# Grouped-query attention on one core: score matmuls as two 64-row tiles, inputs turned by DMA, and a fifth of the exponentials on VectorE

## The chip, the core and the metric

The kernel runs on one core of a Trainium2 chip. A core has a matrix engine (PE, TensorE) that writes only into PSUM, an activation engine (ACT, ScalarE), a vector engine (DVE, VectorE), a general engine (POOL, GpSimd) and a sync engine (SP) that issues transfers. Data lies in SBUF (128 partitions) and, for matmul results, in PSUM (128 partitions, 8 banks of 512 fp32 columns). Engines run side by side and wait for each other through semaphores. Transfers to and from the main memory (HBM) run on 16 DMA engines; SP and POOL issue them here.

The metric is the device time of one execution in microseconds (us), as the median of several runs.

## The reference: what is computed

Eight batches, eight query heads, two key/value heads, 1024 positions, head size 64. Four query heads share one key/value head.

```python
batch, n_q_heads, n_kv_heads, seq, head_dim = (8, 8, 2, 1024, 64)
...
scale = 1.0 / np.sqrt(head_dim)
for g in range(n_kv_heads):
    ...
    scores = scale * np.matmul(q_group, k_group.transpose(0, 1, 3, 2))
    scores_max = np.max(scores, axis=-1, keepdims=True)
    attn = np.exp(scores - scores_max)
    attn = attn / (np.sum(attn, axis=-1, keepdims=True) + 1e-08)
    output[:, q_start:q_end, :, :] = np.matmul(attn, v_group)
```

All inputs and the output are float32. Entries are about 0.1 in size, so scores are small, and both kernels take exp without subtracting the maximum. In total there are 64 (batch, head) pairs with 1024 x 1024 scores each, so 67 million exponentials: 524,288 for each of the 128 partitions.

## The kernel before

Scores are computed transposed: keys on the partitions, queries along the columns. That way the exponentials come out in the layout that the second matmul needs, and no transpose of the probabilities is needed. A *cell* is 128 keys by 512 queries; three cells make a *wave*, which fills one slot of three PSUM banks. Two such slots exist.

```python
qT_pool = ctx.enter_context(tc.tile_pool(name="qTpool", bufs=2 * NPAIR))
pT_pool = ctx.enter_context(tc.tile_pool(name="pTpool", bufs=16))
...
spool = ctx.enter_context(tc.tile_pool(name="spsum", bufs=2, space=bass.MemoryType.PSUM))
opool = ctx.enter_context(tc.tile_pool(name="opsum", bufs=1, space=bass.MemoryType.PSUM))
tpool = ctx.enter_context(tc.tile_pool(name="tpsum", bufs=1, space=bass.MemoryType.PSUM))
```

Inputs are loaded as fp32. PE transposes them, reading only the upper 16 bits of each value (`_hi16`) as bf16; VectorE copies the result out of PSUM. Two heads are turned together, so the 128 partitions of `qT` hold head 2j in the lower 64 and head 2j+1 in the upper 64. The key tile has zeros in the other half, so that a 128-row matmul gives the scores of one head alone.

```python
def transpose_group(stages, lo, name_pool):
    tp = tpool.tile([128, NSC, 128], BF16, name="tpsum")
    for sc in range(NSC):
        nc.tensor.transpose(tp[:, sc, :], _hi16(stages[sc])[:, lo : lo + 2, :], ident)   # L107
    dst = name_pool.tile([128, NSC, 128], BF16, name="xT")
    nc.vector.tensor_copy(out=dst, in_=tp)                                              # L111
    return dst
```

One wave: three score matmuls, then one exponential over 1536 columns on ACT.

```python
def score_wave(gw, qT, kT):
    ...
    sps = spool.tile([128, CPERW, QBS], FP32, name="spsum")
    with tc.high_priority(offset=1 << 20):
        for slot, gc in enumerate(cells):
            ...
            nc.tensor.matmul(                                                           # L183
                sps[:, slot, :],
                lhsT=kT[b][g][side][:, c, :],
                rhs=qT[(b, pair)][:, qb * NQS : (qb + 1) * NQS, :],
                start=True, stop=True,
            )
    pt = pT_pool.tile([128, CPERW, QBS], BF16, name="pt")
    nc.scalar.activation(out=pt[:, 0:n, :], in_=sps[:, 0:n, :], func=AF.Exp, scale=scale)  # L191
    return pt
```

The output of 512 queries takes 32 matmuls. The value tile has a 65th column of ones, so the sum of the exponentials comes with the output and VectorE divides by it.

```python
def output_block(b, pair, side, qb, pts, vt):
    ops = opool.tile([128, NQS, D + 1], FP32, name="opsum")
    ...
    for qs in range(NQS):
        for c in range(NKC):
            nc.tensor.matmul(ops[:, qs, :], lhsT=..., rhs=_hi16(vt[b][g][:, c, :]),      # L204
                             start=(c == 0), stop=(c == NKC - 1))
    rec = recip_pool.tile([128, NQS], FP32, name="rec")
    nc.vector.reciprocal(out=rec, in_=ops[:, :, D])                                     # L214
    ost = ostage_pool.tile([128, NQS, D], FP32, name="ost")
    nc.vector.tensor_tensor(out=ost, in0=ops[:, :, 0:D], in1=..., op=ALU.mult)          # L216
    (nc.gpsimd if (qb + side) % 2 else nc.sync).dma_start(out=..., in_=ost)             # L222
```

The file also holds a function for exponentials on VectorE (`dve_exp_cell`), which nothing calls. The order of instructions on each engine is left to the scheduler of the language layer, with raised priority for the scores.

Of the kernel before, what the change touches and what calls it, by code (L numbers as in the profile page):

```python
# [10 lines left out]
def _hi16(ap: bass.AP) -> bass.AP:  # L11
    b = ap.bitcast(mybir.dt.bfloat16)
    return b[..., 1::2]
# [3 lines left out]
def kernel(  # L17
# [7 lines left out]
    nc = tc.nc  # L25
    FP32 = mybir.dt.float32
    BF16 = mybir.dt.bfloat16
    AF = mybir.ActivationFunctionType
# [3 lines left out]
    G = k.shape[1]  # L32
    HPG = H // G
    NPAIR = H // 2
    NKC = S // 128
    NSC = S // 128
    QBS = 512
    NQB = S // QBS
    NQS = QBS // 128
    CPERW = 3  # L40
    NCELL = 2 * NQB * NKC
    scale = 1.0 / math.sqrt(D)

    VEC_EVERY = 5
    LOG2E = 1.4426950408889634
    EC2 = 0.2385171
    EHH = 1.47456484
    EMM = 0.48179846

    const_pool = ctx.enter_context(tc.tile_pool(name="constp", bufs=1))  # L50

    qstage_pool = ctx.enter_context(tc.tile_pool(name="qstage", bufs=2 * NSC))
    kstage_pool = ctx.enter_context(tc.tile_pool(name="kstage", bufs=2 * NSC))
    vstage_pool = ctx.enter_context(tc.tile_pool(name="vstage", bufs=2 * G))

    qT_pool = ctx.enter_context(tc.tile_pool(name="qTpool", bufs=2 * NPAIR))
    kT_pool = ctx.enter_context(tc.tile_pool(name="kTpool", bufs=2 * 2 * G))

    pT_pool = ctx.enter_context(tc.tile_pool(name="pTpool", bufs=16))

    ostage_pool = ctx.enter_context(tc.tile_pool(name="ostage", bufs=4))
    recip_pool = ctx.enter_context(tc.tile_pool(name="recip", bufs=4))
    vexp_pool = ctx.enter_context(tc.tile_pool(name="vexp", bufs=2))

    spool = ctx.enter_context(tc.tile_pool(name="spsum", bufs=2, space=bass.MemoryType.PSUM))
    opool = ctx.enter_context(tc.tile_pool(name="opsum", bufs=1, space=bass.MemoryType.PSUM))
    tpool = ctx.enter_context(tc.tile_pool(name="tpsum", bufs=1, space=bass.MemoryType.PSUM))

    ident = const_pool.tile([128, 128], BF16)
    make_identity(nc, ident)  # L70

    def load_stage(b):
        kstage = []
        qstage = []
        for sc in range(NSC):
            ks = kstage_pool.tile([128, 2 * G + 1, D], FP32, name="kstage")
            nc.vector.memset(ks[:, 0::2, :], 0.0)  # L77
            nc.sync.dma_start(
                out=ks[:, 1::2, :],
                in_=k[b].rearrange("g (sc p) d -> sc p g d", p=128)[sc],  # L80
            )
            kstage.append(ks)
            qstage.append(qstage_pool.tile([128, H, D], FP32, name="qstage"))
        for j in range(NPAIR):
            eng = nc.gpsimd if j % 2 == 0 else nc.sync
            for sc in range(NSC):
                eng.dma_start(  # L87
                    out=qstage[sc][:, 2 * j : 2 * j + 2, :],
                    in_=q[b, 2 * j : 2 * j + 2].rearrange(
                        "h (sc p) d -> sc p h d", p=128  # L90
                    )[sc],
                )
        vt = []
        for g in range(G):
            vs = vstage_pool.tile([128, NKC, D + 1], FP32, name="vstage")
            nc.vector.memset(vs[:, :, D], 1.0)  # L96
            nc.sync.dma_start(
                out=vs[:, :, 0:D],
                in_=v[b, g].rearrange("(c p) d -> p c d", p=128),
            )  # L100
            vt.append(vs)
        return qstage, kstage, vt

    def transpose_group(stages, lo, name_pool):
        tp = tpool.tile([128, NSC, 128], BF16, name="tpsum")
        for sc in range(NSC):
            nc.tensor.transpose(  # L107
                tp[:, sc, :], _hi16(stages[sc])[:, lo : lo + 2, :], ident
            )
        dst = name_pool.tile([128, NSC, 128], BF16, name="xT")  # L110
        nc.vector.tensor_copy(out=dst, in_=tp)  # L111
        return dst

    def prologue_transposes(qstage, kstage):
        kT = [[None, None] for _ in range(G)]
        qT = [None] * NPAIR
        order = []
        seen = set()
        for j in range(NPAIR):
            g = (2 * j) // HPG  # L120
            if g not in seen:
                seen.add(g)
                order.append(("k", (g, 0)))
                order.append(("q", j))
                order.append(("k", (g, 1)))
            else:
                order.append(("q", j))
        for kind, idx in order:
            if kind == "k":
                g, side = idx  # L130
                kT[g][side] = transpose_group(kstage, 2 * g + 1 - side, kT_pool)
            else:
                qT[idx] = transpose_group(qstage, 2 * idx, qT_pool)
        return qT, kT

    I32 = mybir.dt.int32

    def dve_exp_cell(psum_cell, out_cell):
        sc = scale * LOG2E
        u = vexp_pool.tile([128, QBS], FP32, name="vxu")  # L140
        y = vexp_pool.tile([128, QBS], I32, name="vxy")
        w = vexp_pool.tile([128, QBS], FP32, name="vxw")
        e = vexp_pool.tile([128, QBS], I32, name="vxe")
        with tc.high_priority(offset=1 << 19):
            nc.vector.tensor_scalar(
                out=u, in0=psum_cell, scalar1=sc, scalar2=None, op0=ALU.mult
            )
        nc.vector.tensor_copy(out=y, in_=u)
        nc.vector.tensor_copy(out=w, in_=y)
        nc.vector.scalar_tensor_tensor(  # L150
            out=w, in0=w, scalar=EHH, in1=u, op0=ALU.subtract, op1=ALU.subtract
        )
        nc.vector.tensor_scalar(
            out=e, in0=y, scalar1=127, scalar2=float(1 << 23),
            op0=ALU.add, op1=ALU.mult,
        )
        nc.vector.tensor_tensor(out=w, in0=w, in1=w, op=ALU.mult)
        nc.vector.tensor_scalar(
            out=u, in0=w, scalar1=EC2, scalar2=EMM, op0=ALU.mult, op1=ALU.add
        )  # L160
        nc.vector.tensor_tensor(
            out=out_cell, in0=u, in1=e.bitcast(FP32), op=ALU.mult
        )

    NCELLS = B * NPAIR * NCELL

    def cell_of(gc):
        c = gc % NKC
        qb = (gc // NKC) % NQB
        side = (gc // (NKC * NQB)) % 2  # L170
        pair = (gc // NCELL) % NPAIR
        b = gc // (NCELL * NPAIR)
        return b, pair, side, qb, c

    def score_wave(gw, qT, kT):
        cells = list(range(gw * CPERW, min((gw + 1) * CPERW, NCELLS)))
        n = len(cells)
        sps = spool.tile([128, CPERW, QBS], FP32, name="spsum")
        with tc.high_priority(offset=1 << 20):
            for slot, gc in enumerate(cells):  # L180
                b, pair, side, qb, c = cell_of(gc)
                g = (2 * pair) // HPG
                nc.tensor.matmul(  # L183
                    sps[:, slot, :],
                    lhsT=kT[b][g][side][:, c, :],
                    rhs=qT[(b, pair)][:, qb * NQS : (qb + 1) * NQS, :],
                    start=True,
                    stop=True,
                )
        pt = pT_pool.tile([128, CPERW, QBS], BF16, name="pt")  # L190
        nc.scalar.activation(  # L191
            out=pt[:, 0:n, :], in_=sps[:, 0:n, :], func=AF.Exp, scale=scale
        )
        return pt

    def output_block(b, pair, side, qb, pts, vt):
        g = (2 * pair) // HPG
        h = 2 * pair + side
        ops = opool.tile([128, NQS, D + 1], FP32, name="opsum")
        base = (((b * NPAIR + pair) * 2 + side) * NQB + qb) * NKC  # L200
        for qs in range(NQS):
            for c in range(NKC):
                gc = base + c
                nc.tensor.matmul(  # L204
                    ops[:, qs, :],
                    lhsT=pts[gc // CPERW][
                        :, gc % CPERW, qs * 128 : (qs + 1) * 128
                    ],
                    rhs=_hi16(vt[b][g][:, c, :]),
                    start=(c == 0),  # L210
                    stop=(c == NKC - 1),
                )
# [11 lines left out]
                :, qb * NQS : (qb + 1) * NQS, :  # L224
            ],
            in_=ost,
        )

    NGW = (NCELLS + CPERW - 1) // CPERW
    ready_after = {}  # L230
# [62 lines left out]
```

The softmax here doesn't subtract the row's maximum and nothing guards it: scores larger than these inputs give would overflow.

## Time and profile before

| | before |
|---|---|
| time, median of 3 runs (lowest to highest) | 480.45 us (479.83 to 481.53) |
| span of the profiled execution | 480.1 us |
| matmuls on PE | 5632: 1024 scores, 4096 outputs, 512 transposes |
| ACTIVATE on ACT | 342 |
| instructions on VectorE | 400 |
| moved by DMA | 42.82 MB, mean 89 GB/s |
| granted TensorE clock | 0.998 |

How to read it: "busy" is the time in which an engine has at least one instruction under way. A matmul or an ACTIVATE lasts longer than the distance to the next one, because neighbours overlap in the pipeline; so a mean length times the number can exceed the busy time, and the pace is read from the distance between starts. "Idle before" names what ended an engine's wait. The chain of work that ended last is followed backwards from the end, and shows which engine's work set the time. Lines such as L191 are those of the kernel's file. PE is the matmul part of TensorE, PEld its weight loads.

### The profile page before, as it was taken

The numbers are of one execution on the slowest core, as the hardware profiler recorded it, in microseconds if no ns is written. First come the engines' busy times: TensorE is split into PE (matmuls) and PEld (weight loads), VectorE is DVE, ScalarE is ACT, GpSimd is POOL, SyncE is SP. The second block draws the span as 40 slices with busy tenths as digits, with TensorE's granted clock in tenths as the row PEclk, the third lists the DMA queues.
The fourth block names the chain that finished last, engine by engine and source line by source line (L and its number), as shares of the span: only waits on it lengthen the run. The fifth ranks groups of instructions, "written<-read, shape, count | busy, mean of one in ns | idle before, by whom it ended". The sixth has DMA issues, their size and how long they took to land.

```text
span 480.1 us, 13304 instructions
## 1 busy us (share of the span) xinstructions
PE 443.3 (92%) x5632; PEld 282.6 (59%) x5632; DVE 129.3 (27%) x400; ACT 460.2 (96%) x343; POOL 141.1 (29%) x198
## 2 busy tenths in 40 slices
PE   2999999999999999999999999999999998988895
PEld 1566666666666666666565656656565555555553
DVE  3332233232242323222241312313222111111112
ACT  1699999999999999999999999999999999999996
POOL 9993056128047111830138010111100111101011
PEclk9999999999999999999999999999999999999999
DMA  7997356138157122842148121211212111111111
GB/s 177 218 227 182 79 142 169 45 90 219 35 125 198 47 55 58 197 109 58 35 115 206 34 56 46 67 34 35 56 45 58 40 39 35 46 34 34 46 34 45
DMA packets 109883, 42.82 MB, mean 89 GB/s; under 512 B 105728, under 2 KB 105728, under 8 KB 109824
## 3 DMA queue, kind: packets, MB, share of 16 engines
q1 hardware_dynamic: 102656, 25.18, 24.8%
q0 software_dynamic: 7168, 16.79, 11.1%
q8 instruction: 44, 0.72, 0.6%
q14 instruction: 15, 0.12, 0.1%
HBM read 25.17 MB, written 16.78 MB: 87 GB/s over the span
## 4 chain that ended last, share of the span: by engine, by line
ACT 72%; PE 21%; issue 3%; POOL 1%; DMA 1%; DVE 1%; POOLq 0%
ACT pt L191 72%; PE spsum L183 13%; PE opsum L204 6%; PE tpsum L107 2%; POOL qstage L87 1%; DMA qstage<-in_q_dram 1%; DVE ost L216 0%; DVE xT L111 0%; DVE rec L214 0%; POOL ident masks.py:199 0%; POOL ident masks.py:197 0%; POOLq masks.py:199 0%; POOLq L277 0%
## 5 line engine op out<-in xcount | busy, mean ns | idle before, releaser
L191 ACT ACTIVATE pt<-spsum 128x1536 bf16<-128x1536 f32 x342 | 458.9, 1706 | 14.6 <-PE spsum L183 14.6
L183 PE MATMUL spsum<-xT 128*128 128x512 bf16 x1024 | 278.2, 380 | 23.5 <-ACT pt L191 19.0
L204 PEld LDWEIGHTS <-pt 128*128 128x128 bf16 x4096 | 174.0, 98 | 75.9 <-DVE ost L216 16.9
L204 PE MATMUL opsum<-vstage,pt 128*128 128x65 bf16 x4096 | 191.1, 195 | 1.1 <-DVE ost L216 1.0
L183 PEld LDWEIGHTS <-xT 128*128 128x128 bf16 x1024 | 98.5, 97 | 94.2 <-issue 35.8
L222 POOL DMA_DIRECT2D out_dram<-ost x64 | 48.3, 755 | 316.1 <-DVE ost L216 283.6
L214 DVE RECIPROCAL rec<-opsum 128x4 f32<-128x4 f32 x128 | 23.4, 183 | 309.2 <-PE opsum L204 300.4
L87 POOL DMA_DIRECT2D qstage<-in_q_dram x128 | 92.2, 723 | 18.4 <-PE tpsum L107 12.8
L216 DVE TENSOR_TENSOR ost<-opsum,rec 128x256 f32<-128x256 f32 x128 | 53.8, 421 | 3.7 <-DVE rec L214 0.2
L111 DVE COPY xT<-tpsum 128x1024 bf16<-128x1024 bf16 x64 | 43.6, 681 | 32.9 <-PE tpsum L107 20.7
L107 PE MATMUL tpsum<-ident,kstage 128*128 128x128 bf16 x256 | 28.5, 226 | 5.4 <-DMA kstage<-in_k_dram 5.3
L107 PE MATMUL tpsum<-ident,qstage 128*128 128x128 bf16 x256 | 27.4, 225 | 3.3 <-DVE xT L111 1.6
L107 PEld LDWEIGHTS <-kstage 128*128 128x128 bf16 x256 | 18.9, 101 | 14.0 <-issue 5.7
L107 PEld LDWEIGHTS <-qstage 128*128 128x128 bf16 x256 | 18.6, 101 | 9.8 <-issue 2.8
L77 DVE MEMSET kstage<- 128x192 f32 x64 | 13.5, 218 | 2.3 <-PE tpsum L107 0.9
L191 ACT ACT_TABLE_LOAD x1 | 1.3, 1283 | 0.7 <-PEq L277 0.7
L96 DVE MEMSET vstage<- 128x8 f32 x16 | 0.9, 65 | 0.0
masks.py:199 POOL TENSOR_SCALAR_AFFINE_SELECT ident<-ident 128x128 bf16<-128x128 bf16 x1 | 0.3, 307 | 0.1
masks.py:197 POOL MEMSET ident<- 128x128 bf16 x1 | 0.2, 205 | 0.3 <-POOLq L277 0.3
L277 POOL MEMSET const-float32-0.0<- 128x1 f32 x1 | 0.1, 99 | 0.2 <-issue 0.2
L277 POOL MEMSET const-bfloat16-1.0<- 128x1 bf16 x1 | 0.1, 102 | 0.0
L277 POOL MEMSET const-uint8-127<- 128x1 uint8 x1 | 0.1, 102 | 0.0
(1 smaller groups left out, 0.1 us busy)
## 6 DMA issues: line engine op xcount, KB each, us to landing
qstage<-in_q_dram POOLq DMA_DIRECT2D x128, 64.0 KB, 3.7
qstage<-in_q_dram SPq DMA_DIRECT2D x128, 64.0 KB, 3.4
out_dram<-ost SPq DMA_DIRECT2D x64, 128.0 KB, 1.9
out_dram<-ost POOLq DMA_DIRECT2D x64, 128.0 KB, 2.3
kstage<-in_k_dram SPq DMA_DIRECT2D x64, 64.0 KB, 2.7
vstage<-in_v_dram SPq DMA_DIRECT2D x16, 256.0 KB, 3.1
```

The costliest lines, as they stand in the source:

```text
L77: nc.vector.memset(ks[:, 0::2, :], 0.0)
L87: eng.dma_start(out=qstage[sc][:, 2 * j : 2 * j + 2, :], in_=q[b, 2 * j : 2 * j + 2].rearrange("h (sc p) d -> sc p h d", p=128)[sc],)
L96: nc.vector.memset(vs[:, :, D], 1.0)
L107: nc.tensor.transpose(tp[:, sc, :], _hi16(stages[sc])[:, lo : lo + 2, :], ident)
L111: nc.vector.tensor_copy(out=dst, in_=tp)
L183: nc.tensor.matmul(sps[:, slot, :], lhsT=kT[b][g][side][:, c, :], rhs=qT[(b, pair)][:, qb * NQS : (qb + 1) * NQS, :], start=True, stop=True,)
L191: nc.scalar.activation(out=pt[:, 0:n, :], in_=sps[:, 0:n, :], func=AF.Exp, scale=scale)
L204: nc.tensor.matmul(ops[:, qs, :], lhsT=pts[gc // CPERW][:, gc % CPERW, qs * 128 : (qs + 1) * 128], rhs=_hi16(vt[b][g][:, c, :]), start=(c ...
L214: nc.vector.reciprocal(out=rec, in_=ops[:, :, D])
L216: nc.vector.tensor_tensor(out=ost, in0=ops[:, :, 0:D], in1=rec.unsqueeze(2).to_broadcast([128, NQS, D]), op=ALU.mult,)
L222: (nc.gpsimd if (qb + side) % 2 else nc.sync).dma_start(out=out[b, h].rearrange("(qs p) d -> p qs d", p=128)[:, qb * NQS : (qb + 1) * NQS, :],
L277: nc = _bacc.Bacc("TRN2", target_bir_lowering=False, num_devices=1)
```

## The change

It is a rewrite of the whole kernel around the same idea (transposed scores, a 65th column of ones). Its parts:

- **Even and odd queries as two tiles.** The 1024 x 64 queries of one head are seen as 512 x 128: row r holds query 2r in the first 64 numbers and query 2r+1 in the last. Turned, the lower 64 partitions hold the even queries and the upper 64 the odd ones. A score pair is then two matmuls of 64 rows each, one on each half of the array, into two PSUM banks. Keys are turned in the same way, and a second copy with swapped halves lets either half see any keys. The zero padding is gone.
- **q and k turned by DMA.** POOL issues transfers that cast fp32 to bf16 into scratch tensors in HBM; SP issues DMA transposes from there into SBUF. The transposes on PE, their PSUM bank and the copies out of it go. The freed space makes three score slots of two banks, and two banks for outputs.
- **One in five exponentials on VectorE.** For the last pair of every third head and the last two pairs of the others, VectorE writes `A*score + B`, rounded to uint16: read as bf16, that is a power of two times a straight line between powers. A quadratic correction in the seven mantissa bits follows in four steps, all in 16 bits.
- **Planned order.** A small model in the file (`Plan`, with fixed durations) lays down the order of scores, exponentials, VectorE steps and output matmuls; the scheduler of the language layer is switched off (`manual_schedule`).

The core of the diff, with cuts (all lines of the old kernel shown above are removed):

```diff
-from concourse.masks import make_identity
+class Plan:
+    ...   # durations as constants; lays down self.ev, the order of all events
+    NSLOT = 3
+    LOOK = 2
+    QAHEAD = 5
+    def ndve(j):
+        return 2 if j % 3 else 1
+    ...
+    yp = ctx.enter_context(tc.tile_pool(name="yp", bufs=5))
+    spsum = ctx.enter_context(tc.tile_pool(name="spsum", bufs=NSLOT, space=bass.MemoryType.PSUM))
+    opsum = ctx.enter_context(tc.tile_pool(name="opsum", bufs=1, space=bass.MemoryType.PSUM))
+    ctx.enter_context(tc.manual_schedule())
+    ...
+    def cast_q(j):
+        t = dram.tile([HS, 2 * D], BF16, name=f"qd{j}")
+        nc.gpsimd.dma_start(out=t.rearrange(...), in_=q[b, h].rearrange(...))
+    def cast_v(b, g):
+        for par in range(2):
+            nc.gpsimd.dma_start(out=va[...], in_=v[b, g].rearrange(...)[par])
+    def turn_k(b, g):
+        t = kt[b][g]
+        nc.sync.dma_start_transpose(out=t[:, 0:1, :], in_=kd[(b, g)])
+        nc.sync.dma_start(out=t[D : 2 * D, 1, :], in_=t[0:D, 0, :])
+        nc.sync.dma_start(out=t[0:D, 1, :], in_=t[D : 2 * D, 0, :])
+    def turn_q(j):
+        t = qp.tile([128, 1, HS], BF16, name="qt")
+        nc.sync.dma_start_transpose(out=t, in_=qd[j])
+    plan = Plan(NJ, ndve, LOOK, NSLOT, 2, 8)
+    CAST_AHEAD = 8
+    TURN_AHEAD = QAHEAD
+    ...
+    for _, kind, x, j, c in plan.ev:
+        if kind == "score":
+            sp = spsum.tile([128, 2, HS], FP32, name="sp")
+            for half in range(2):
+                lo = half * D
+                slot = 0 if par == half else 1
+                nc.tensor.matmul(sp[:, half, :],
+                    lhsT=t[lo : lo + D, slot, cc * 128 : (cc + 1) * 128],
+                    rhs=qt[j][lo : lo + D, 0, :], start=True, stop=True)
+        elif kind == "act":
+            p = pp.tile([128, 2, HS], BF16, name="pt")
+            nc.scalar.activation(out=p, in_=sps.pop((j, c)), func=AF.Exp, scale=scale)
+        elif kind == "dpass":          # first pass: PSUM fp32 -> uint16
+            nc.vector.tensor_scalar(out=yt[j][:, c - (8 - n), :, :], in0=sps.pop((j, c)),
+                scalar1=EXP_A, scalar2=EXP_B, op0=ALU.mult, op1=ALU.add)
+        elif kind == "dstep":          # four steps on all n pairs of the head
+            if x == 0:
+                nc.vector.tensor_scalar(out=ut[j][:, 0:n], in0=y, scalar1=127, scalar2=None,
+                    op0=ALU.bitwise_and)
+            elif x == 1:
+                nc.vector.tensor_scalar(out=vt[j][:, 0:n], in0=ut[j][:, 0:n],
+                    scalar1=-EXP_R, scalar2=EXP_K, op0=ALU.add, op1=ALU.mult)
+            elif x == 2:
+                nc.vector.tensor_tensor(out=vt[j][:, 0:n], in0=ut[j][:, 0:n], in1=vt[j][:, 0:n], op=ALU.mult)
+            else:
+                nc.vector.tensor_tensor(out=y, in0=y, in1=vt[j][:, 0:n], op=ALU.add)
+        elif kind == "pv":             # eight output matmuls at a time
+            ops[j] = opsum.tile([128, 2, 512], FP32, name="ops")
+            nc.tensor.matmul(ops[j][:, par, qs * (D + 1) : (qs + 1) * (D + 1)],
+                lhsT=p_of(j, ci)[:, par, qs * 128 : (qs + 1) * 128],
+                rhs=va[:, b * G + h // HPG, ci, :], start=(ci == 0), stop=(ci == 7))
+        else:                          # norm, once a head
+            nc.vector.reciprocal(out=rec, in_=o[:, :, :, D])
+            nc.vector.tensor_tensor(out=..., in0=o[:, :, :, 0:D], in1=..., op=ALU.mult)
+            nc.sync.dma_start(out=..., in_=ost)
```

## The prediction

> **What bounds the kernel now.** I read the page's busy shares first, then the chain of work that ended last, then the groups of instructions, and last a stretch of the timeline.
>
> Busy shares, and the chain:
>
> ```profile
> PE 443.3 (92%) x5632; PEld 282.6 (59%) x5632; DVE 129.3 (27%) x400; ACT 460.2 (96%) x343; POOL 141.1 (29%) x198
> ...
> ACT 72%; PE 21%; issue 3%; POOL 1%; DMA 1%; DVE 1%; POOLq 0%
> ```
>
> ACT, which takes every exponential, fills 96% of the span and 72% of the chain. PE is close behind, VectorE (DVE) has 350 us to spare. The groups, with the times ACT and PE take for one piece of work:
>
> ```profile
> L191 ACT ACTIVATE pt<-spsum 128x1536 bf16<-128x1536 f32 x341 | 458.4, 1709 | 14.6 <-PE spsum L183 14.6
> L183 PE MATMUL spsum<-xT 128*128 128x512 bf16 x1024 | 278.2, 380 | 23.5 <-ACT pt L191 19.0 <-DVE xT L111 0.8
> L204 PE MATMUL opsum<-vstage,pt 128*128 128x65 bf16 x4096 | 191.1, 195 | 1.1 <-DVE ost L216 1.0
> ...
> L216 DVE TENSOR_TENSOR ost<-opsum,rec 128x256 f32<-128x256 f32 x128 | 53.8, 421 | 3.7 <-DVE rec L214 0.2
> ...
> L111 DVE COPY xT<-tpsum 128x1024 bf16<-128x1024 bf16 x64 | 43.6, 681 | 32.9 <-PE tpsum L107 20.7 <-PE spsum L183 12.1
> ...
> L214 DVE RECIPROCAL rec<-opsum 128x4 f32<-128x4 f32 x128 | 23.4, 183 | 309.2 <-PE opsum L204 300.4 <-issue 8.6
> ...
> L191 ACT ACTIVATE pt<-spsum 128x512 bf16<-128x512 f32 x1 | 0.9, 874 | 0.0
> ```
>
> ACT's 14.6 us of idle time is almost all the start (its first exponential begins at 13.8 us). From then on 458.4 us for 341 pieces is 1.344 us each. One ACTIVATE lasts longer than that (about 1.73 us), so neighbours overlap. From the two shapes (874 ns at 512 columns, 1727 ns at the 1536-column median) a column costs (1727 - 874)/1024 = 0.833 ns, and 447 ns are latency. The pace of 1344 ns is 1280 for the columns and at most 64 on top.
>
> The stretch of the timeline shows what else runs at that pace (start, length, then the instructions merged):
>
> ```profile
> 201.10 0.81 PE L183 MATMUL spsum<-xT 128*128 128x512 bf16 x3
> ...
> 201.75 0.72 PE L204 MATMUL opsum<-vstage,pt 128*128 128x65 bf16 x17
> ...
> 202.44 0.81 PE L183 MATMUL spsum<-xT 128*128 128x512 bf16 x3
> ```
>
> Score bursts start 1.34 us apart, locked to ACT. Narrow stretches around them put an ACTIVATE at 202.01 to 203.74, the score burst that reuses its slot at 203.79 to 204.60, and the next ACTIVATE on that slot at 204.70. That is a ring: 1.73 + 0.05 + 0.81 + 0.10 = 2.69 us for two slots, 1.34 each. So ACT is held both by its own columns and by the two score slots in PSUM, which are just as slow. Inside the bursts scores start (0.81 - 0.38)/2 = 0.215 us apart, and output matmuls (0.72 - 0.195)/16 = 0.033 us apart.
>
> **What the Trainium skill says.**
>
> 1. "TensorE: Matmul & The Clock Gate", Part 3 (packing small matmuls): matmuls whose operands lie in different row groups run side by side, about 4 ns apart. The kernel before has only 128-row matmuls, so its trace shows nothing of this.
> 2. "VectorE: DVE Perf Modes", the perf-mode tier table: at 2048 columns a 16-bit scalar operation in SBUF takes 693 ns (four columns a cycle), a 16-bit two-tensor one 1224 ns (two a cycle); fp32 from PSUM gets one column a cycle. The trace agrees where it can: 256 fp32 columns from PSUM took 421 ns, at 0.96 GHz 267 + 154; 1024 bf16 columns from PSUM 681 = 533 + 148. No SBUF-source row exists.
> 3. The same page, the three transpose paths: a 128x128 DMA transpose takes 1309 ns. Not in this trace, which transposes on PE.
> 4. "SBUF — State Buffer", "Who interferes with whom": VectorE in the four-a-cycle mode and GpSimd lock each other out. The trace has no such pair to show it.
>
> **The change, part by part.**
>
> *ACT.* 64 heads make 512 score pairs of 128 keys by 1024 queries. One pair a head when the head's number divides by 3 (22 heads), two otherwise (42), go to VectorE: 22 + 84 = 106. ACT keeps 406. Each costs 1024 x 0.833 + at most 64 = 917 ns, in all 372 us where 459 stood: 87 us less. There are three slots instead of two: (874 + 427) + 0.05 + about 0.38 for the pair + 0.10 is 1.83 us over three, 0.61 each, well under 0.917. The ring of before no longer binds, unless VectorE sits on a slot.
>
> *PE.* The 512 transposes go (28.5 + 27.4 us of busy time in their two groups). If the two 64-row halves run together, a pair takes about 0.22 us: 512 x 0.22 = 113 us where 1024 x 0.215 = 220 stood. Output matmuls stay 4096 x 0.033 = 135 us. The recorded order of PE changes 459 times between the two kinds; if the array empties each time, I charge the tail of a matmul, 377 - 215 = 162 ns, so 74 us at most. Sum 322 us: not the bound.
>
> *VectorE.* This is where work is added, and it is much.
>
> - First pass, 1024 fp32 columns from PSUM: 1067 + 154 = 1.22 us x 106 = 129 us.
> - Four SBUF steps a head: two at four columns a cycle, two at two. By the skill's figures at two pairs: 2 x 0.693 + 2 x 1.224 = 3.83 us x 42 = 161 us. At one pair, with the same fixed part (about 0.16 us): 2 x 0.43 + 2 x 0.69 = 2.24 us x 22 = 49 us. These are estimates.
> - Normalising, now once a head: reciprocal about 0.187, multiply of 512 columns 533 + 154 = 0.687; 0.874 x 64 = 56 us, where the old one took 77.
>
> Sum 395 us. The memsets and PSUM copies of before (58 us) are gone. Steps of a head wait on each other: the reciprocal and the multiply that needs it stand 217 ns apart in the trace where 183 is the reciprocal, so 34 ns lie between. If half of the 490 instructions pay that, 8 us: about 403.
>
> So **the bound moves from ACT (372) to VectorE (403)**. Beside work, two ends: before the first scores lie a cast, a transpose and a copy in series, which I set at 10 us from what single DMAs took before (2.7 to 3.7 us each); behind the last multiply lies one store, 3 us as before (477 to 480). That is 416. On top comes coupling: slots are reused in fixed order, so a pair waiting for VectorE blocks the third pair after it, and all engines follow one fixed order. I add 2%, 8 us. Prediction **424 us**.
>
> **Rivals.**
>
> *ACT stays the bound.* If the SBUF steps have less fixed cost than the skill's figure and waits hide, VectorE falls to about 375 and the end is 12 + 372 + 6 for the last head's outputs = 390, or 400 with some coupling. For it: no SBUF row contradicts it. Against: both engines at 372 in a fixed order can hardly both run full.
>
> *The tiles do not overlap on PE.* Then a pair takes 0.43 us, 220 + 135 + 74 = 429 us of PE and a time near 450. For it: nothing in this trace shows overlap. Against: the skill's measurement.
>
> *DMA takes the place.* 80 transposes of 512x128 on one queue; at 4 x 1309 ns each, 419 us in series, as long as the kernel, and late ones would stop PE: 435 to 455. Against: the figure for one block holds a fixed latency that a larger transfer pays once, and q is fetched five heads ahead. GpSimd's 112 casting DMAs can also be held up by VectorE, or hold it up (they cost it 0.72 us each before, 81 us in all).
>
> *VectorE does not reach its fast modes* on mixed uint16 and bf16. At one column a cycle the four steps cost about 4 x 2.29 = 9.2 us a two-pair head and the kernel over 590 us. Unlikely, but the only way I see to a slower kernel.
>
> **Range and chances.** 400 is ACT as bound with coupling; 455 is PE in series, DMA trouble or strong coupling. Each of the last three I hold at about one in ten, fast modes missing at one in twenty. Faster than 471 us needs only that nothing doubles: 0.92; within 2%: 0.03; slower: 0.05.
>
> **What would show it.** In the profile after: VectorE busy near 95% and ahead of ACT in the chain; ACT about 372 us busy, with gaps ended by scores that waited for VectorE's slots; first pass 1.22 us, two-pair steps near 0.69 and 1.22 us; the two halves of a pair starting a few ns apart; ACT's first exponential near 10 to 12 us. I am wrong on the mechanism if ACT is above 97% and VectorE under 90%, if score halves stand 0.215 us apart, or if PE's waits end with the transposed q.

## The result, and the profile after

The changed kernel takes 429.49 us (median of 4 runs, 425.94 to 430.09) where the one before takes 480.14. The ratio is 0.892, with a 95% interval of 0.888 to 0.896. Ratios here and below leave out executions more than 1.5% above the fastest of the same kernel; where no ratio is given, what was left did not allow one.

First the busy shares, the DMA row of the 40 slices and the chain that ended last, from the page of the changed kernel:

```profile
PE 333.9 (78%) x5120; PEld 196.9 (46%) x5120; DVE 375.4 (88%) x491; ACT 380.6 (89%) x407; POOL 66.7 (16%) x116
...
DMA  8999999999952225233232424323242222331112
...
DVE 70%; PE 12%; issue 9%; DMA 5%; POOL 2%; ACT 2%; ACTq 0%; POOLq 0%
```

VectorE went from 27% to 88% busy and took the chain over from ACT. But neither engine is near 100%, and for the first 11 of the 40 slices (118 us) the DMA engines are nearly full. The groups of the same page (count, then busy us and mean ns, then idle time before):

```profile
L358 ACT ACTIVATE pt<-sp 128x1024 bf16<-128x1024 f32 x406 | 379.3, 1041 | 37.7 <-PE sp L348 37.6
...
L365 DVE TENSOR_SCALAR yt<-sp 128x1024 uint16<-128x1024 f32 x106 | 128.9, 1216 | 29.0 <-PE sp L348 28.9
...
L409 DVE TENSOR_TENSOR ost<-ops,rec 128x512 f32<-128x512 f32 x64 | 44.2, 691 | 2.2
```

The first pass lasts 1.22 us and the normalising multiply 0.69 us, as worked out. Both engines that share the exponentials wait for PE's scores: ACT 37.7 us, VectorE 29.0.

Where these waits lie is seen by cutting off both ends. This is the stretch from 150 to 370 us of the changed kernel, the busy time and count of each engine, then granted clock, DMA share and GB/s:

```profile
core 0: us, PE busy (x) PEld busy (x) DVE busy (x) ACT busy (x) POOL busy (x), PEclk, DMA share, GB/s
150.00:370.00 220.00, 182.86 (x2862) 108.12 (x2860) 209.36 (x274) 211.01 (x226) 0.00 (x0) 0.98 0.33 75
```

In the middle VectorE is 95.2% busy and ACT 95.9%: two engines side by side, with 10.6 and 9.0 us of gaps in 220. On the timeline of ACT the pattern repeats every 18.33 us, which is three heads and 19 exponentials:

```profile
244.00 6.61 ACT L358 ACTIVATE pt<-sp 128x1024 bf16<-128x1024 f32 x7 [0.36 <-PE sp L348]
250.84 11.13 ACT L358 ACTIVATE pt<-sp 128x1024 bf16<-128x1024 f32 x12 [0.23 <-PE sp L348]
262.33 1.94 ACT L358 ACTIVATE pt<-sp 128x1024 bf16<-128x1024 f32 x2 [0.36 <-PE sp L348]
```

From 244.00 to 262.33 are 6.11 us a head. Starts inside a run stand 0.904 us apart, so ACT alone would need 19 x 0.904 = 17.18 us of the 18.33.

The clock granted to PE is not full all the time. The trace has stretches of 3.4 us at half of it, in which a score matmul lasts 0.61 us instead of 0.39. Two of them lie in this window; this is one, then a stretch without any:

```profile
186.00:189.40 3.40, 3.40 (x45) 2.15 (x41) 2.09 (x3) 2.43 (x3) 0.00 (x0) 0.50 0.50 121
...
160.00:180.00 20.00, 16.53 (x268) 9.83 (x267) 19.22 (x28) 19.42 (x22) 0.00 (x0) 1.00 0.37 74
```

Nineteen exponentials that run over such a stretch take about 19.2 us instead of 18.33. So counts over a window mix the order with the clock, and the pace between such stretches is the cleaner measure. Why the clock was halved is not shown.

The whole span then splits by VectorE like this: 19.2 us until its first pass, 389.9 us from there to the end of its last step (409.1), and 18.8 us in which it only normalises the last heads.

### The profile page after: what moved, and what is told of

Read it like the earlier page. It is cut to its first block, busy times and chain, and to the rows that moved or that the text cites. A ratio compares the mean times of both kernels' runs of the same rounds, so it can differ in the third digit from the quotient of the medians.

```text
span 427.9 us, 12083 instructions
## 1 busy us (share of the span) xinstructions
PE 333.9 (78%) x5120; PEld 196.9 (46%) x5120; DVE 375.4 (88%) x491; ACT 380.6 (89%) x407; POOL 66.7 (16%) x116
## 4 chain that ended last, share of the span: by engine, by line
DVE 70%; PE 12%; issue 9%; DMA 5%; POOL 2%; ACT 2%; ACTq 0%; POOLq 0%
DVE yt L365 23%; DVE vt L384 11%; DVE yt L388 11%; DVE ost L409 10%; DVE ut L374 8%; PE ops L396 7%; PE sp L348 5%; DVE vt L379 4%; DMA qt<-qd 4%; DVE rec L407 3%; ACT pt L358 2%; DMA qd<-in_q_dram 1%; POOL va L275 1%; POOL qd L257 1%; POOL kd L267 0%
## 5 line engine op out<-in xcount | busy, mean ns | idle before, releaser
L358 ACT ACTIVATE pt<-sp 128x1024 bf16<-128x1024 f32 x406 | 379.3, 1041 | 37.7 <-PE sp L348 37.6
L348 PE MATMUL sp<-qt,kt 64*128 64x512 bf16 x1024 | 183.3, 394 | 70.3 <-ACT pt L358 28.1
L396 PE MATMUL ops<-va,pt 128*128 128x65 bf16 x3248 | 164.3, 197 | 19.5 <-DVE ost L409 19.4
L365 DVE TENSOR_SCALAR yt<-sp 128x1024 uint16<-128x1024 f32 x106 | 128.9, 1216 | 29.0 <-PE sp L348 28.9
L396 PE MATMUL ops<-va,yt 128*128 128x65 bf16 x848 | 112.0, 196 | 0.0
L348 PEld LDWEIGHTS <-kt 64*128 64x128 bf16 x1024 | 47.3, 94 | 133.7 <-issue 98.0
L388 DVE TENSOR_TENSOR yt<-yt,vt 128x2048 uint16<-128x2048 uint16 (+1 forms) x64 | 66.4, 1038 | 1.4
L384 DVE TENSOR_TENSOR vt<-ut,vt 128x2048 bf16<-128x2048 uint16 (+1 forms) x64 | 66.3, 1035 | 0.9
L396 PEld LDWEIGHTS <-yt 128*128 128x128 bf16 x848 | 62.1, 99 | 0.0
L409 DVE TENSOR_TENSOR ost<-ops,rec 128x512 f32<-128x512 f32 x64 | 44.2, 691 | 2.2
L275 POOL DMA_DIRECT2D va<-in_v_dram x32 | 25.2, 792 | 10.7 <-DMA va<-in_v_dram 4.8
```

Of the source, the lines that this page charges most:

```text
L275: nc.gpsimd.dma_start(out=va[:, b * G + g, par * (NC // 2) : (par + 1) * (NC // 2), 0:D], in_=v[b, g].rearrange("(c p two) d -> two p c d" ...
L348: nc.tensor.matmul(sp[:, half, :], lhsT=t[lo : lo + D, slot, cc * 128 : (cc + 1) * 128], rhs=qt[j][lo : lo + D, 0, :], start=True, stop=True,)
L358: nc.scalar.activation(out=p, in_=sps.pop((j, c)), func=AF.Exp, scale=scale)
L365: nc.vector.tensor_scalar(out=yt[j][:, c - (8 - n), :, :], in0=sps.pop((j, c)), scalar1=EXP_A, scalar2=EXP_B, op0=ALU.mult, op1=ALU.add,)
L384: nc.vector.tensor_tensor(out=vt[j][:, 0:n], in0=ut[j][:, 0:n], in1=vt[j][:, 0:n], op=ALU.mult)
L388: nc.vector.tensor_tensor(out=y, in0=y, in1=vt[j][:, 0:n], op=ALU.add)
```

## The experiments

Theory V says that VectorE's work bounds the middle. The rivals: ACT does, PE does, or the coupling of the engines does, whatever VectorE's work is.

### 1. The four steps on VectorE left out

```diff
         elif kind == "dstep":
+            continue
```

This leaves out the quadratic correction, so the exponentials of VectorE are coarser.

> The four SBUF steps on VectorE are left out (the exponentials there stay a straight line between powers of two, so the result is coarser); everything else and every order is kept. Theory V (VectorE bounds the steady part, 6.1 us a head): 206 us of VectorE work go, ACT becomes the bound with 406 x 0.904 = 367 us, so 22 us of start + 367 + about 12 of end = about 400 us, ACT without gaps. Rival C (the coupling of slots and the fixed order set the pace, whatever VectorE does): 420 us or more. Rival P (PE sets it): unchanged, 428 us.

Measured: 412.10 to 422.12 us over four runs. The same stretch of this run's trace:

```profile
150.00:370.00 220.00, 191.38 (x2988) 112.79 (x2985) 106.83 (x136) 217.72 (x236) 0.00 (x0) 1.00 0.34 80
```

VectorE fell to 49% busy, and ACT got 236 exponentials done instead of 226, only 4.4% more, at 99% busy. Here no half-clock stretch lies in the window; the pace of 19 exponentials is 17.72 us instead of 18.33:

```profile
262.76 17.54 ACT L358 ACTIVATE pt<-sp 128x1024 bf16<-128x1024 f32 x19 [0.18 <-PE sp L348]
280.48 17.54 ACT L358 ACTIVATE pt<-sp 128x1024 bf16<-128x1024 f32 x19 [0.17 <-PE sp L348]
```

So halving VectorE's work buys 0.61 us in 18.33 and no more, for ACT stands right behind. It also takes away waits for VectorE elsewhere, so this run alone can't tell VectorE's work from the coupling. The expected 400 us missed: it had 22 us of start and 12 of end in it (measured: first exponential at 23.2 us, 8.8 us behind the last one), but not the 17 us in all by which starts on ACT still stand further apart than 0.904 us.

### 2. Four constants of the plan set to measured values

```diff
-M_PAIR = 240
-M_SWITCH = 120
-M_PV = 41
-M_ACT = 920
+M_PAIR = 228
+M_SWITCH = 90
+M_PV = 33
+M_ACT = 904
```

No instruction is added or removed; only their order changes.

> Only four constants of the plan are set to what this study's profiles show (pair 228 ns, change of tile shape 90, output matmul 33, exponential 904), which moves the order of PE and of the others. Theory V (VectorE bounds at 6.11 us a head): 425 to 430, as before. Rival C (the order's coupling costs the 20 us of gaps on ACT): 410 to 420.

Measured: 417.63 to 426.22 us over four runs, ratio 0.8725 to the kernel before (0.867 to 0.878), against 0.892 for the changed kernel; the median of all four, 423.51, lies between the two expectations; experiment 9 repeats the order in five runs that lie close together. The same stretch, and two periods of ACT:

```profile
150.00:370.00 220.00, 186.55 (x2940) 112.11 (x2937) 215.81 (x284) 217.07 (x234) 0.00 (x0) 1.00 0.35 80
...
295.04 17.66 ACT L358 ACTIVATE pt<-sp 128x1024 bf16<-128x1024 f32 x19 [0.23 <-PE sp L348]
312.91 17.66 ACT L358 ACTIVATE pt<-sp 128x1024 bf16<-128x1024 f32 x19 [0.22 <-PE sp L348]
```

234 exponentials instead of 226, with the same work on VectorE: both engines above 98% busy, three heads in 17.88 us. Part of the 234 is the clock, for this window has no half-clock stretch. By the undisturbed pace a better order alone brings 0.45 of the 0.61 us that leaving out the steps brought. Rival C is right for most of the gap in the middle; what is left, 0.16 us, returns in experiment 8.

Which wait shrank can be read from the waits for whom, first of the changed kernel, then of this run (us in total, times, longest):

```profile
PE ops L396 <- DVE ost L409: 19.4, 41, 1.0
```

```profile
PE ops L396 <- DVE ost L409: 3.9, 17, 0.2
```

PE stands before the first output matmul of a head until VectorE has normalised the head before, because there is one output tile. (Its waits for the score slots that VectorE reads rose meanwhile, from 19.0 to 27.8 us.) PE works in fixed order, so the next scores stand behind it. The timeline of the changed kernel shows the whole path:

```profile
260.46 0.69 DVE L409 TENSOR_TENSOR ost<-ops,rec 128x512 f32<-128x512 f32 x1
...
261.21 0.40 PE L396 MATMUL ops<-va,pt 128*128 128x65 bf16 x7 [0.64 <-DVE ost L409]
...
261.84 0.89 PE L348 MATMUL sp<-qt,kt 64*128 64x512 bf16 x4
...
262.33 2.95 ACT L358 ACTIVATE pt<-sp 128x1024 bf16<-128x1024 f32 x3 [0.36 <-PE sp L348]
...
263.98 1.22 DVE L365 TENSOR_SCALAR yt<-sp 128x1024 uint16<-128x1024 f32 x1 [0.37 <-PE sp L348]
```

The multiply ends at 261.15. PE, idle for 0.64 us, first runs the outputs, then the scores, and both ACT and then VectorE wait for these. A second output tile would test this directly, but PSUM's eight banks are taken (three slots of two, and two for outputs), so it was not tried.

### 3. 96 instead of 106 pairs on VectorE

```diff
-        return 2 if j % 3 else 1
+        return 2 if j % 2 else 1
```

> 96 instead of 106 pairs on VectorE (one or two a head in turn). VectorE loses 10 x 1.22 us and about 17 us of steps, 29 in all; ACT gains 9 us. Theory V: per head VectorE 5.7 and ACT 6.5 x 0.904 = 5.9 us, so ACT sets a pace of 5.9 instead of 6.1 and the time falls by 5 to 14 us, to 415 to 424. Rival A (ACT is already the bound): 9 us slower, 437.

Measured: 426.56 us, ratio 0.8885 (0.884 to 0.893), not told apart from the changed kernel by the intervals. Four heads take 24.15 us, 6.04 each, close under 6.11. ACT took 9 us more work, VectorE lost 29, and the result is a draw: rival A's 437 us did not come, nor theory V's 415 to 424. The added work went into ACT's gaps: from 100 us on, its starts lose 8.2 us to gaps instead of 22.5. In the first 100 us they lose 13.5 instead of 7.3; PE's clock was halved there for 10 us on end.

### 4. No exponential on VectorE

```diff
-        return 2 if j % 3 else 1
+        return 0
```

> No exponentials on VectorE; all 512 pairs on ACT, the rest of the change kept. Theory V with ACT next in line: 512 x 0.904 = 463 us + 22 of start + about 8 of end = 493 us, so slower than the kernel before by 2 to 3%: all that the change gains would then hang on the VectorE share. If the tiles, DMA transposes and three slots were worth much by themselves, it would lie clearly under 480 us.

Measured: 513.55 us, ratio 1.069 (1.065 to 1.074). The tiles, DMA transposes, third slot and order together gain nothing without VectorE's share; the kernel is then slower than before. Beyond the expected 493 lie 20 us by which starts on ACT stood further apart than its own pace. They come with the clock: it was granted at 0.91 in this run and in the others of this kernel, in 27 stretches at half. One without and one with it:

```profile
176.00:195.00 19.00, 12.72 (x176) 6.52 (x173) 2.69 (x6) 19.00 (x22) 0.00 (x0) 1.00 0.25 65
...
195.60:199.00 3.40, 3.40 (x52) 2.47 (x49) 0.00 (x0) 3.40 (x5) 0.00 (x0) 0.50 0.33 77
```

Of the 20.7 us, 20.0 lie within 2 us before to 4 us behind such a stretch; elsewhere ACT keeps its 0.904 us. At full clock the sum of 493 us would thus stand, still above the 480 of before (an estimate from these two figures).

### 5. Score matmuls over all 128 rows

```diff
-        nc.sync.dma_start_transpose(out=t[:, 0:1, :], in_=kd[(b, g)])
-        nc.sync.dma_start(out=t[D : 2 * D, 1, :], in_=t[0:D, 0, :])
-        nc.sync.dma_start(out=t[0:D, 1, :], in_=t[D : 2 * D, 0, :])
+        w = kw.tile([128, 1, HS], BF16, name="kw")
+        nc.sync.dma_start_transpose(out=w, in_=kd[(b, g)])
+        for par in range(2):          # into a tile with zeros in the other half
+            for half in range(2):
+                nc.sync.dma_start(out=t[half * D : half * D + D, 2 * par + half, :],
+                                  in_=w[par * D : par * D + D, 0, :])
 ...
-                    lhsT=t[lo : lo + D, slot, cc * 128 : (cc + 1) * 128],
-                    rhs=qt[j][lo : lo + D, 0, :],
+                    lhsT=t[:, 2 * par + half, cc * 128 : (cc + 1) * 128],
+                    rhs=qt[j][:, 0, :],
```

> Score matmuls over all 128 rows again, with zeros in the unused half of the keys (two more small copies and memsets for each key tile); the rest kept. PE then needs 1024 x 0.215 = 220 us for scores instead of about 115, in all about 355 us and no change of tile shape. Theory V: PE has the room, time within 2% of the changed kernel (428 to 437 us). Rival P (the two tiles are what makes the gain): 5% or more slower, 450 us or above.

Measured: 437.41 to 447.43 us, between the two expectations. The extra copies and memsets fell into the crowded first 120 us, so this did not settle it. It was repeated with paced transfers (experiment 6):

> 128-row score matmuls with zero-padded keys again, now with the paced casts, so that the crowded transfers of the first 130 us do not blur the comparison (zeros written by POOL, two more copies for each key tile). Against the paced run with two tiles (422 us): theory V says PE has room, 422 to 428, steady pace within 1% of 18.33 us for three heads. Rival P: 435 or more.

Measured: 426.11 us, ratio 0.886 (0.884 to 0.888), against 0.878 of the paced run with two tiles: 1% slower. Of these 4.2 us, 3.1 are a later first exponential (18.7 us against 15.6). The stretch of the middle, for the paced run with 128 rows, then with two tiles:

```profile
150.00:370.00 220.00, 205.88 (x2794) 127.28 (x2838) 209.72 (x275) 210.93 (x227) 60.02 (x117) 1.00 0.63 113
```

```profile
150.00:370.00 220.00, 181.69 (x2862) 107.50 (x2862) 210.46 (x276) 211.96 (x228) 53.12 (x99) 0.99 0.64 108
```

PE went from 83% to 94% busy, and ACT did 227 exponentials instead of 228; the two-tile run has one half-clock stretch in the window, the other none. The undisturbed pace is 18.53 us for three heads instead of 18.33, 1.1% slower. So the two tiles do run together and free PE, but in this kernel PE has the room: rival P falls. In the faster order of experiment 2, where PE is busier (186.6 us of the 220, not 182.9), the tiles were not taken out.

### 6. The start: order and pace of the transfers

The start of the changed kernel on the sync engine:

```profile
4.17 1.24 SPq L282 DMA_TRANSPOSE kt<-kd  x1
...
10.73 0.53 SPq L283 DMA_DIRECT2D kt<-kt  x1
...
11.32 0.57 SPq L284 DMA_DIRECT2D kt<-kt  x1
...
11.94 5.25 SPq L288 DMA_TRANSPOSE qt<-qd  x4
```

The copy at 10.73 waits for the transpose of k, more than 6 us behind its issue. The first q, which needs none of this, is turned only after it. One run turns q first; another also paces the casts:

```diff
     def turn_k(b, g, j):
         nc.sync.dma_start_transpose(out=t[:, 0:1, :], in_=kd[(b, g)])
+        turn_q(j)                       # both runs
         nc.sync.dma_start(out=t[D : 2 * D, 1, :], in_=t[0:D, 0, :])
 ...
-    QAHEAD = 5                          # from here on the paced run alone
-    CAST_AHEAD = 8
+    QAHEAD = 4
+    CAST_AHEAD = 5
 ...
         if j + CAST_AHEAD < NJ:
+            nc.gpsimd.tensor_copy(out=tiny, in_=p[:, 0, 0:1])
             cast_for(j + CAST_AHEAD)
```

The paced run also issues the first casts of v after those of q and k.

> Of the paced run only the order on the sync engine: q of the first head is turned ahead of the two key copies; casts are issued as in the changed kernel. If the order made the gain of the start: first exponential near 16 us, time 421 to 424. If the crowded DMA engines made the late start: first exponential at 19 to 22 us, 425 to 429.

> Transfers only: the first head's q is turned ahead of the two swapped key copies, four heads of q are turned ahead instead of five, and POOL issues the casts of a head only when an exponential five heads earlier is done (a copy of one column on POOL waits for it), so that casts no longer fill the DMA engines over the first 130 us. Theory S (the cast traffic costs the start about 10 us and the first 100 us a few stalls): first exponential at 12 to 14 us instead of 22, time 412 to 417. Rival L (the start is a chain of fixed latencies and later heads now come late): within 1% of the changed kernel, 425 to 432, or slower.

Measured: with q first 427.09 us, ratio 0.888 (0.884 to 0.891), first exponential at 19.5 us; paced 421.94 us, ratio 0.878 (0.875 to 0.881), first exponential at 15.6 us instead of 22.0. The issues of transfers (count, KB each, median us to landing) show what changed, first in the changed kernel, then paced:

```profile
qd<-in_q_dram POOLq DMA_DIRECT2D x64, 128.0 KB, 6.3
```

```profile
qd<-in_q_dram POOLq DMA_DIRECT2D x64, 128.0 KB, 3.4
```

Nothing ever held POOL's casts back to the head that needed them: each has a scratch tensor of its own, so POOL issued all of them within the first 105 us. The transfers that mattered stood in that crowd. Order alone gives 2.5 of the 6.4 us, as the second case of its expectation has it; the rest comes from pacing together with the later casts of v and one head less of q turned ahead, which were not parted. Theory S holds in direction, though the time stayed 5 us and the first exponential 1.6 us above its ranges.

### 7. The scheduler of the language layer instead of the plan

```diff
-    ctx.enter_context(tc.manual_schedule())
```

> The planned order is given up on: the scheduler of the language layer is switched on again and reorders the same instructions (it puts an independent instruction between a reciprocal and its multiply, and between steps of two heads). Rival O (the planned order is a large part of the gain): 445 us or more. Theory V (the work on VectorE sets the pace, any sound order serves): within 2%, 420 to 437.

Measured: 460.24 us, ratio 0.957 (0.954 to 0.959): rival O holds. Yet late in this run 19 exponentials take 18.25 us, the pace of the changed kernel. The loss lies early: 59 exponentials start in the first 100 us instead of 79, and the clock is halved for 48 us in all, most of it early. The waits name it, VectorE's multiply waiting for a store to free its buffer, up to 12.9 us at a time:

```profile
DVE ost L408 <- DMA out_dram<-ost: 30.9, 5, 12.9
```

So here the plan's worth shows in the crowded phase, not in the steady pace. Whether paced casts would mend it was not tried.

### 8. Keeping dependent VectorE instructions apart

```diff
+M_DEP = 117
 ...
-                    cands.append((max(tD, chains[0][2]), 2, "chain", None))
+                for n, ch in enumerate(chains[:2]):
+                    cands.append((max(tD, ch[2]), 2 + n, "chain", n))
 ...
-                            ch[2] = tD
+                            ch[2] = tD + M_DEP
```

Reciprocal and multiply become two events, and the four constants of experiment 2 (and VectorE's own, lowered to match the overlap) are in it.

> As the run with four measured constants, and besides the plan charges 117 ns for a VectorE instruction right behind the one it needs (a pair that depends stands 34 ns apart, one that does not overlaps by 83) and may work on two heads' steps in turn; reciprocal and multiply are laid out apart. Dependent neighbours fall from 210 to about 134. Theory V: 76 x 0.117 = 9 us less on VectorE, so 5 to 9 us under the run with the constants alone. Rival C: no difference to that run.

Measured: 422.36 us, ratio 0.876 (0.872 to 0.880), against 0.8725 (0.867 to 0.878) with the constants alone. The time shows no gain, and the trace shows where it went. From 150 to 370 us, 86 neighbours stand 34 ns apart instead of 122, and ACT's period is 17.71 us for three heads instead of 17.88:

```profile
264.15 17.54 ACT L365 ACTIVATE pt<-sp 128x1024 bf16<-128x1024 f32 x19 [0.17 <-PE sp L355]
281.86 17.54 ACT L365 ACTIVATE pt<-sp 128x1024 bf16<-128x1024 f32 x19 [0.17 <-PE sp L355]
```

That is the pace of experiment 1, where VectorE had half the work: at 17.71 us VectorE no longer bounds. PE's waits for the slots that VectorE reads fell from 27.8 to 8.1 us, which speaks for theory V in this last 0.17 us, though other events moved too. But the clock was halved in seven stretches of 3.4 us here, in three with the constants alone, and three heads that run over one take about 18.7 us; over the whole window that makes 6.03 us a head. All runs of this order show it (granted clock 0.968 to 0.974, against 0.979 to 0.991). Why this order brings more of these stretches is open.

### 9. Pacing and order together

> Both found improvements together: paced casts with the first head's q turned early, and the plan with measured constants that keeps dependent VectorE instructions apart. If the start (6 us) and the steady pace (18.33 to 17.72 us for three heads, ACT with 0.17 us of gap for 19 exponentials) add up: 428 - 7 - 13 = 406 to 410, ACT above 92% busy and ahead of VectorE in the chain. If each gain only hides the same wait: 417 or more.

> Paced casts and the four measured constants, without keeping dependent VectorE instructions apart. Theory V: steady pace 17.88 us for three heads, so 3 to 4 us above the run with both (409 to 414). Rival: the same time.

Measured: 412.09 us with dependent instructions apart, 2 us above its range, ratio 0.858 (0.855 to 0.860); 408.35 us with the four constants alone, ratio 0.849 (0.847 to 0.851). Pacing and order add up, because they mend different stretches. That the simpler version is the faster of the two was not expected: it had been put 3 to 4 us above the other. Its pace of three heads is the slower one (17.88 us, against 17.71), but it has two half-clock stretches, both at the very end, where the other has seven. It beats both kernels: 5% under the changed one, 15% under the one before. The page of that best run:

```profile
PE 329.5 (81%) x5120; PEld 197.7 (49%) x5120; DVE 372.8 (92%) x491; ACT 378.3 (93%) x407; POOL 95.2 (23%) x175
...
DVE 75%; issue 10%; DMA 5%; ACT 4%; PE 4%; SPq 0%; ACTq 0%; POOLq 0%
```

ACT and VectorE are both at 92 to 93% of the whole span, start and tail included.

## Why the prediction was right, point by point

The predicted 424 us stand against 429.49, inside the range of 400 to 455. Most terms held; three were mis-sized, and their errors cancelled almost whole. The direction and the engine that leads the chain were foreseen; that the total came within 1.3% was in good part luck.

- **ACT.** Predicted at most 917 ns a piece and no binding ring; measured 904 ns between starts, 367 us in all. Right. (A single one lasts 1.04 us, not the 874 + 427 ns put into the ring of slots.)
- **PE.** Pairs were put at 0.22 us. The timeline of the changed kernel:

```profile
200.45 0.39 PE L348 MATMUL sp<-qt,kt 64*128 64x512 bf16 x2
...
200.77 0.36 PE L396 MATMUL ops<-va,pt 128*128 128x65 bf16 x6
...
201.49 0.23 PE L396 MATMUL ops<-va,yt 128*128 128x65 bf16 x2
...
201.65 0.39 PE L348 MATMUL sp<-qt,kt 64*128 64x512 bf16 x2
```

Two matmuls in 0.39 us, where one alone lasts 0.386: the halves start 4 ns apart at the median (2 to 29). This agrees with the Trainium skill, "TensorE: Matmul & The Clock Gate", Part 3, which says 4 ns. Pairs follow each other at 0.225 us. The change of tile shape costs less than the charged 162 ns: 83 ns more on the way to the outputs (308 ns between starts where 225 is the pace) and 93 on the way back (126 where 33 is). At 459 changes that is 40 us, not 74.

- **VectorE's work.** The sum of lengths was put at 395 us and is 396.1. The fast modes hold on mixed uint16 and bf16: at 2048 columns 0.68 to 0.69 us for one input and 1.21 to 1.23 for two, as "VectorE: DVE Perf Modes", the perf-mode tier table, has it for bf16. (The rival without these modes did not come; by its own 9.2 us, half of that for one pair, VectorE alone would have needed about 670 us, not 590.)
- **What failed: "If half of the 490 instructions pay that, 8 us: about 403."** Dependent neighbours do stand 34 ns apart, 210 of 490. But 252 others, which need not wait for the one ahead, start about 83 ns before it has ended. The trace before had this too, and it was overlooked; here a copy stands between a reciprocal and its multiply, and each starts 0.08 us early:

```profile
59.82 0.18 DVE L214 RECIPROCAL rec<-opsum 128x4 f32<-128x4 f32 x1 [3.16 <-PE opsum L204]
59.92 0.66 DVE L111 COPY xT<-tpsum 128x1024 bf16<-128x1024 bf16 x1
60.50 0.41 DVE L216 TENSOR_TENSOR ost<-opsum,rec 128x256 f32<-128x256 f32 x1
```

The same instructions then need 375.4 us of busy time, not 403. That is the 375 of the rival "ACT stays the bound", reached by overlap and not by shorter steps. So VectorE did not clearly outgrow ACT: it leads the chain as foreseen, 70% to 2%, but in the middle both are equally busy, and the pace there was set by the order (experiment 2) more than by VectorE's work.

- **What failed: the start, "which I set at 10 us".** VectorE began at 19.2 us and ACT at 22.0. The first cast of k had landed by 4.2 us, but its transpose held the copy until 10.7, and copy and q landed at 16.1 and 18.5; casts in the crowd took 6.3 us at the median, not the 2.7 to 3.7 that single transfers took before. The rival "DMA takes the place" was right for the start, in a form not thought of: transposes are not slow in general (a 512x128 one lands in 3.5 us at the median), but casts sent early crowd them. With paced casts the copies land at 13.0 us, so 10 us was too low even without the crowd.
- **What failed: the end, one store of 3 us.** VectorE's steps run two heads ahead, so they end at 409.1 us, and 18.8 us follow in which ACT, PE and the last four normalisations finish the job.
- **Coupling, 8 us.** The middle runs at 6.11 us a head where the same work in a better order ran at 5.96, so 64 x 0.15 = 9.6 us: the size was right. The cause is right in part. PE does wait for slots that VectorE holds, as the prediction has it, 19.0 us in 39 waits; it also waits 19.4 us behind the single output tile, which the prediction did not see. In experiment 2 the second wait all but went while the first grew, and the pace got better, which speaks for the output tile; it is not isolated.

In sum: +9 at the start, +16 at the end, and VectorE with its coupling took 390 us where 403 + 8 = 411 had been put: 424 + 9 + 16 - 21 = 428. The errors at both ends and the one in the middle are of like size and opposite sign.

**What the change owes its gain to.** The exponentials taken from ACT are all of it (experiment 4). The tiles are worth about 1% (experiment 5), the order of transfers and of PE cost 5% that could be had back (experiment 9). What the DMA transposes and the third slot are worth each was not tried.

## What to carry to other kernels

When work is moved from a full engine to an idle one, stop where both need the same time: beyond that, look for the order and the waits between them, which cost 2.5% of the pace here (18.33 us against 17.88) with no engine above 96%. Data fetched ahead should also be held back to the use that needs it, for transfers issued too early delay the first ones. And a plan with fixed durations is worth measuring again on its own profile: four constants gave 2% here, and 3% with paced transfers. Before two orders are compared by their time, compare the clock that PE was granted, or the pace at full clock: without that, experiments 4 and 8 would be read wrongly.

## What the runs showed of the hardware that was not expected

- Independent VectorE instructions overlap by about 83 ns in the changed kernel, dependent ones stand 34 ns apart: 117 ns between the two orders.
- PE's clock was halved in stretches of 3.4 us, or of several times that on end, in most runs; a score matmul over 64 rows then lasts 0.61 us instead of 0.39. Their number differed with the order: 27 with no exponential on VectorE, two in the best run.
- Changing between 64-row and 128-row matmuls costs 83 and 93 ns.
- VectorE's four-a-cycle steps beside GpSimd's descriptors, of which "SBUF — State Buffer", "Who interferes with whom", warns, lost little here. The slowest 2048-column mask took 957 ns against a median of 686. The four slowest of these steps, 733 to 957 ns, each ran beside a transfer that POOL was issuing, so the trace agrees in kind; POOL was busy for 66.7 us in all.
